# Routed experts of 128 tokens by gathered rows, with dense expert products of 384 columns

## The chip, the cores and the metric

The kernel runs on one core of a Trainium2 chip. The metric is the time of one execution on the device in microseconds, the median of several runs. Beside it stands one execution taken by the hardware profiler, whose trace gives every duration below.

## What is computed

One block with attention and a layer of routed experts (`peer`), then two blocks of another kind. The change touches `peer` alone. It has 512 tokens of width 1024, 16384 experts of one row each (`peer_u`, `peer_v`), eight heads that choose 16 experts for each token:

```
s1, i1 = lax.top_k(s[:, :, 0], K)
s2, i2 = lax.top_k(s[:, :, 1], K)
cand = (s1[..., :, None] + s2[..., None, :]).reshape(T, H, K * K)
sc, ci = lax.top_k(cand, K)
e1 = jnp.take_along_axis(i1, ci // K, axis=-1)
e2 = jnp.take_along_axis(i2, ci % K, axis=-1)
idx = e1 * PEER_NKEYS + e2
g = jax.nn.softmax(sc, axis=-1)
...
a = jnp.einsum('cd,chkd->chk', xc, u[ic])
act = (jax.nn.gelu(a.astype(jnp.float32)) * gc).astype(xc.dtype)
return jnp.einsum('chk,chkd->cd', act, v[ic])
```

So each token needs 128 rows of `u` and 128 rows of `v`.

## The kernel before

Most tokens are done densely: for all 128 groups of 128 experts (called experts in the loops) TensorE multiplies the group's tile of `u` with the tokens' features, the activations are masked with a matrix G of gate values, and products with `v` add them up. Every f32 product is three products in the f32r type (`mm3`, lines 177 to 179): weights and tokens are split into a high and a low part. The weight stream `WS.load` brings a tile of 128 x 1024 numbers over SyncE's queue, ScalarE casts it to `wh` (line 99), and VectorE or GpSimd subtracts to get `wl` (line 100). Three tiles of each kind are kept.

The first `TG` = 64 tokens are done by rows instead: GpSimd issues indirect DMAs that bring one row to each of 128 partitions (64 tokens, two halves of their choices), 64 gathers of `u` and 64 of `v`, each 512 KB (line 1373). VectorE multiplies the `u` rows with the tokens and sums (line 1390), later weights and adds the `v` rows into `av` (line 1409). The dense products have 512 - 64 = 448 columns.

`peer` runs in this order. The first loop goes over 128 up-experts, 24 products each. Beside it run generators, advanced by credits: `route` picks the experts, tile by tile of 128 tokens (four tiles), on VectorE: maxima and indices of scores, then sums of candidates, then lookups of the chosen indices by comparing with 0 to 15, multiplying and reducing (lines 1503 to 1507). ScalarE makes the Exp of `ge` (line 1488). When routing has ended, `build_g` makes G in steps of eight tokens: marks in f16 on VectorE (lines 1529 to 1535), 16 products of 128 columns on TensorE (line 1552), a scaled copy on ScalarE, and stores to DRAM as `g_d`. One `u` gather goes with each expert from there on. GpSimd makes `wl` for experts below `RES` = 104, VectorE for the others. The activations of experts below `RES` go to DRAM (`a_d`), the others stay in SBUF.

The second loop goes over the 128 down-experts: load G (`gt`) and activations (`at`), multiply (line 1319), split into `ah` and `al` (lines 215, 216), 24 products into eight PSUM banks `v`. VectorE makes all `wl`. The `v` gathers run beside it, with four row tiles. The last three experts' products are put off to a tail, after which two products of 64 columns for each bank fold `av` in.

TensorE's instructions in the first loop, and the `u` gathers, are held to program order (`keep_in_program_order`); a planner orders the rest for each engine. All engines run their own queue in order. A credit is about a microsecond and a half of VectorE's work in `route` and a step in `build_g`.

## Time and profile before

| | us |
|---|---|
| median of 3 runs | 3810.53 |
| lowest, highest | 3807.4, 3816.54 |
| profiled execution, its own time | 3815.04 |
| span of its trace | 3813.3 |
| TensorE busy in the span | 3712.7 (97%) |
| VectorE busy | 2128.6 (56%) |
| ScalarE busy | 1434.0 (38%) |
| GpSimd busy | 678.3 (18%) |
| mean granted TensorE clock | 0.979 of 2.4 GHz |

Busy times are shares of the whole span; matmuls overlap, so a busy TensorE is not one at its peak. What a stage is worth is read from that stage: a table by stretch shows busy time, number of instructions, granted clock, the busy share of the 16 DMA engines and the bytes moved. In the trace's names PE is TensorE, PEld its weight loads, DVE VectorE, ACT ScalarE, POOL GpSimd. The expert layer takes the time from about 600 to 2017 us of the span; the two blocks behind it last to the end.

### The profile page before, as it was taken

The page shows a single profiled execution, that of the slowest core. Times are in us where ns is not written, and L with a number is a line of the kernel's source. Part 1 is how long each engine was busy: PE and PEld are TensorE (multiplying, and loading weights), DVE is VectorE, ACT ScalarE, POOL GpSimd, SP SyncE. Part 2 cuts the span into 40 slices and gives each one's busy share as a digit, 9 for nine tenths or more (in the row PEclk, how much of TensorE's full clock was granted, in tenths as well). Part 3 has the DMA queues.
Part 4 walks back from the last instruction along what each step waited for, and adds up shares of the span by engine and source line. Part 5 has one row for each costly group of instructions (what it writes and reads, how often), then busy time and mean ns, then how long its engine had stood idle before and what let it go on. Part 6 is the DMA issues. An engine that isn't in the chain of part 4 may idle for free.

```text
span 3813.3 us, 46424 instructions
## 1 busy us (share of the span) xinstructions
PE 3712.7 (97%) x17947; PEld 3083.4 (81%) x17947; DVE 2128.6 (56%) x3507; ACT 1434.0 (38%) x2174; POOL 678.3 (18%) x407
## 2 busy tenths in 40 slices
PE   8999999998999999999999999999999999999998
PEld 7876568887888999999997866778887876878887
DVE  4436555993899658644446364454434554455333
ACT  4444433332566433333333444233223344333222
POOL 1000101454556425100000000121101000022100
PEclk9999899999999999999999999999999999999999
DMA  3124022443678878765553332532233233443232
GB/s 122 56 80 162 18 93 99 144 143 131 247 286 303 324 250 319 269 206 201 204 183 126 115 110 94 189 120 100 95 113 113 89 127 99 139 146 114 99 118 76
DMA packets 208022, 574.12 MB, mean 151 GB/s; under 512 B 20324, under 2 KB 53800, under 8 KB 207800
## 3 DMA queue, kind: packets, MB, share of 16 engines
q1 hardware_dynamic: 189336, 504.00, 38.7%
q0 software_dynamic: 18464, 67.15, 4.9%
q8 instruction: 141, 2.31, 0.2%
q14 instruction: 81, 0.66, 0.1%
HBM read 480.07 MB, written 90.96 MB: 150 GB/s over the span
## 4 chain that ended last, share of the span: by engine, by line
PE 57%; DVE 2%; DMA 2%; issue 1%; POOL 1%; ACT 1%; DVEq 0%; POOLq 0%
PE ps L177 13%; PE ps L179 13%; PE ps L178 13%; PE v L178 4%; PE v L177 4%; PE v L179 4%; DMA nv<-in_vr,gx 2%; PE o L414 1%; PE s L391 1%; PE pss L243 1%; PE tp L408 1%; POOL nv L1373 1%; PE o L773 0%; DVE xk L364 0%; PE bc L261 0%
## 5 line engine op out<-in xcount | busy, mean ns | idle before, releaser
L99 ACT CAST wh<-wr 128x1024 fp32r<-128x1024 f32 x599 | 629.7, 1052 | 1572.6 <-PE ps L178 816.0
L177 PE MATMUL ps<-hnh,wh 128*128 128x512 f32 (+1 forms) x2616 | 1017.7, 392 | 29.7 <-ACT hnh L316 16.0
L179 PE MATMUL ps<-hnh,wl 128*128 128x512 f32 (+1 forms) x2616 | 1011.7, 387 | 7.2 <-POOL wl L100 7.1
L178 PE MATMUL ps<-hnl,wh 128*128 128x512 f32 (+1 forms) x2616 | 1009.8, 386 | 0.0
L100 DVE TENSOR_TENSOR wl<-wr,wh 128x1024 fp32r<-128x1024 f32 x485 | 600.8, 1239 | 666.4 <-ACT wh L99 655.3
L177 PEld LDWEIGHTS ps<-hnh,wh 128*128 128x128 f32 x2616 | 499.3, 191 | 119.1 <-ACT hnh L316 17.0
L179 PEld LDWEIGHTS ps<-hnh,wl 128*128 128x128 f32 x2616 | 497.1, 190 | 95.7 <-POOL wl L100 8.5
L178 PEld LDWEIGHTS ps<-hnl,wh 128*128 128x128 f32 x2616 | 497.3, 190 | 82.2 <-DVE hnl L320 1.7
L100 POOL TENSOR_TENSOR wl<-wr,wh 128x1024 fp32r<-128x1024 f32 x114 | 305.8, 2688 | 533.4 <-ACT wh L99 519.6
L178 PE MATMUL v<-al,wh 128*128 128x448 f32 x1024 | 375.5, 367 | 2.2 <-DVE al L216 2.2
L179 PE MATMUL v<-ah,wl 128*128 128x448 f32 x1024 | 371.5, 363 | 0.0
L177 PE MATMUL v<-ah,wh 128*128 128x448 f32 x1024 | 370.8, 363 | 0.0
L178 PEld LDWEIGHTS v<-al,wh 128*128 128x128 f32 x1024 | 192.1, 188 | 17.1 <-DVE al L216 3.2
L177 PEld LDWEIGHTS v<-ah,wh 128*128 128x128 f32 x1024 | 191.8, 187 | 17.3
L179 PEld LDWEIGHTS v<-ah,wl 128*128 128x128 f32 x1024 | 192.2, 188 | 13.7
L674 POOL TENSOR_TENSOR sg<-sg,bcs 128x512 f32<-128x512 f32 x44 | 75.3, 1712 | 378.4 <-ACT sg L673 378.1
L1554 ACT ACTIVATE gs<-pg 128x512 f32<-128x512 f32 x112 | 120.7, 1193 | 44.3 <-PE pg L1552 44.3
L178 PE MATMUL ps<-hl,wh 128*128 128x512 f32 x352 | 137.0, 389 | 0.0
L177 PE MATMUL ps<-hh,wh 128*128 128x512 f32 x352 | 137.0, 389 | 0.0
L179 PE MATMUL ps<-hh,wl 128*128 128x512 f32 x352 | 137.0, 389 | 0.0
L237 POOL TENSOR_TENSOR sqa<-sqa,sq 128x512 f32<-128x512 f32 x30 | 45.8, 1527 | 510.2 <-DMA xd<-xk 476.1
L177 PE MATMUL ps<-wh,hnh 128*128 128x512 f32 (+1 forms) x320 | 126.2, 398 | 6.6 <-ACT hnh L316 6.6
(492 smaller groups left out, 5289.3 us busy)
## 6 DMA issues: line engine op xcount, KB each, us to landing
wr<-in_pu SPq DMA_DIRECT2D x128, 512.0 KB, 3.7
wr<-in_pv SPq DMA_DIRECT2D x125, 512.0 KB, 3.6
wr<-in_wgu SPq DMA_DIRECT2D x88, 512.0 KB, 3.4
g_d<-gs SPq DMA_DIRECT2D x64, 448.0 KB, 5.9
gt<-g_d SPq DMA_DIRECT2D x32, 896.0 KB, 5.8
wr<-in_wgate SPq DMA_DIRECT2D x48, 512.0 KB, 3.6
a_d<-ga SPq DMA_DIRECT2D x52, 448.0 KB, 3.5
at<-a_d SPq DMA_DIRECT2D x52, 448.0 KB, 4.5
```

Of the source, the lines that this page charges most:

```text
L99: nc.scalar.copy(hi, raw)
L100: eng.tensor_tensor(lo, raw, hi.bitcast(F32), OP.subtract)
L177: self.pe(nc.tensor.matmul(out, w[0], x[0], start=start, stop=False))
L178: self.pe(nc.tensor.matmul(out, w[0], x[1], start=False, stop=False))
L179: self.pe(nc.tensor.matmul(out, w[1], x[0], start=False, stop=stop))
L237: (eng or nc.vector).tensor_tensor(parts[0], parts[0], sq, OP.add)
L243: m = self.nc.tensor.matmul(p[:, i * NT + t:i * NT + t + 1], a, self.ones[:, 0:1], start=j == 0, stop=j == len(parts) - 1)
L391: nc.tensor.matmul(s[:, 0:n], q[:, t * P:n], k[:, 0:n], start=i == 0, stop=False)
L408: nc.tensor.transpose(tp[:, (t - b) * P:(t - b + 1) * P], pr[j, t][:, b * P:(b + 1) * P], self.ident)
L414: nc.tensor.matmul(o[j * 64:j * 64 + 64, b * P:S], heads[j][1](b), pts[j], start=first and b == 0, stop=last and b == NT - 1)
L674: nc.gpsimd.tensor_tensor(t, t, bc, OP.mult)
L1554: nc.scalar.mul(gs[:, :, t0 + h:t0 + h + 4].rearrange("p e t -> p t e"), p, 1.0 / GS)
```

## The change

`TG` becomes 128: the whole first tile of 128 tokens is done by rows, one token to a partition, 128 gathers of `u` and 128 of `v`. The dense products have 384 columns, and `build_g` has 48 steps in place of 56. The tables for the gathers are ready after the first routed tile, and the gathers run from there in one stream (`gather`, 260 steps: fetch, and four steps later the product) through both loops, paced by `NU_C` for each up-expert (0.4 while routing, 0.7 while `build_g` runs, 2.0 after) and `NV_C` = 1.35 for each down-expert, with six row tiles. All are held to program order. In the first loop GpSimd makes `wl` of every expert, in the second of every other one. Routing looks indices up in f16: comparing and multiplying 2048 elements as before, then four halving adds in place of a reduction. The Exp of `ge` comes after the first lookup and is held to program order. 112 experts' activations in place of 104 go through DRAM. Credits for an expert: 3.2 in routing (of 41 for a tile, 45 before, with 3.4), 0.85 in `build_g` (1.3 before).

```diff
@@ setup_late
-        self.ii = cp.tile([P, TG], F32, name="ii")
-        nc.vector.tensor_tensor(self.ii, self.ident[:, 0:TG], self.ident[:, TG:P], OP.add)
+        self.fold = []
+        for n in GROUPS:
+            if n == P:
+                self.fold.append(self.ident)
+                continue
...
@@ peer
-        xt = hp.tile([P, D], F32, name="xt")
+        xts = [hp.tile([P, D], F32, name=f"xt{n}") for n in GROUPS]
...
-        for i in range(2):
-            p = self.ps(name="xt")
-            for k in range(4):
-                for h in range(2):
-                    nc.tensor.matmul(p[h * TG:h * TG + TG, k * P:k * P + P], xs[4 * i + k][:, 0:TG],
-                                     self.ident, start=True, stop=True)
-            nc.scalar.copy(xt[:, i * S:i * S + S], p)
+        for i, (n, b0, _) in enumerate(group_cols()):
+            for j in range(2):
+                p = self.ps(name="xt")
+                for k in range(4):
+                    nc.tensor.matmul(p[0:n, k * P:k * P + P], xs[4 * j + k][:, b0:b0 + n], self.ident, start=True,
+                                     stop=True)
+                for q in range(0, P, n):
+                    nc.scalar.copy(xts[i][q:q + n, j * S:j * S + S], p[0:n])
...
-        near = self.gather_u(vp, sp, xt)
+        near = self.gather(vp, xts)
+        self.near_ready = False
...
-            wu.eng = nc.gpsimd if e < RES else nc.vector
+            wu.eng = nc.gpsimd
             wu.prefetch(2)
...
             else:
-                next(near, None)
                 credit += BG_C
+            if self.near_ready:
+                ncredit += NU_C[0 if not routed else 1 if gen is not None else 2]
+                while ncredit >= 1.0:
+                    next(near)
+                    ncredit -= 1.0
...
+            wv.eng = nc.gpsimd if n % 2 else nc.vector
+            wv.prefetch(2)
+            ncredit += NV_C
+            while ncredit >= 1.0:
+                next(near, None)
+                ncredit -= 1.0
             if n < P - VT:
                 for d in range(KD):
                     self.mm3(dense[d], wv.next(), (ah, al), n == 0, False)
-                if n % 5 and not far and next(near, None) is None and n >= P - RES:
-                    es.close()
-                    vq = self.pool(es, "near")
-                    av = vq.tile([P, D], F32, name="av")
-                    near = self.gather_v(vq, av)
-                    far = True
-                elif far and n % 5:
-                    next(near, None)
...
-            nc.tensor.matmul(acc[d][:, 0:TG], av[:, d * P:d * P + P], self.ii, start=False, stop=True)
+            for i, (m, b0, _) in enumerate(group_cols()):
+                nc.tensor.matmul(acc[d][:, b0:b0 + m], self.near_v[i][:, d * P:d * P + P], self.fold[i], start=False,
+                                 stop=b0 + m == TG)
...
+    def near_tables(self, vp, qp, em, ge):
+        nc = self.nc
+        nt = vp.tile([P, 2, TG], F32, name="nt")
+        whole = GROUPS == (P,)
+        gf = nt if whole else qp.tile([P, 2, P], F32, tag="cd", name="gf", bufs=1)
+        nc.vector.scalar_tensor_tensor(gf[:, 0], em[:, 0], float(P), em[:, 1], OP.mult, OP.add)
+        nc.vector.tensor_copy(gf[:, 1], ge.rearrange("p h k -> p (h k)"))
...
         self.near_i = vp.tile([P, TG], I32, name="gx")
+        nc.vector.tensor_copy(self.near_i, nt[:, 0])
+        self.near_g = nt[:, 1]
+        self.near_ready = True
+
+    def gather(self, vp, xts):
...
+        def fetch(src, j):
+            w = vp.tile([P, D], F32, tag="nr", name="nr", bufs=NR)
+            i = nc.gpsimd.indirect_dma_start(
+                out=w[:], out_offset=None, in_=self.a[src],
+                in_offset=bass.IndirectOffsetOnAxis(ap=self.near_i[:, j:j + 1], axis=0))
             self.tc.keep_in_program_order(i)
+            return w
         rows = []
+        for n in range(2 * TG + NL):
+            if n < 2 * TG:
+                rows.append(fetch("ur" if n < TG else "vr", n % TG))
+            j = n - NL
+            if 0 <= j < TG:
                 u = rows.pop(0)
+                nc.vector.scalar_tensor_tensor(u, u, 1.0, xts[group[j]], OP.mult, OP.mult, accum_out=a[:, j:j + 1])
+                if j == TG - 1:
+                    nc.scalar.activation(a, a, AF.Gelu_apprx_tanh)
+                    nc.vector.tensor_tensor(a, a, self.near_g, OP.mult)
+            elif j >= TG:
+                j -= TG
+                w = rows.pop(0)
...
+                    nc.vector.scalar_tensor_tensor(av, w, a[:, j:j + 1], av, OP.mult, OP.add)
             yield 1
...
@@ route
-                tf = qp.tile([P, 8, 2, 16], F32, tag="tf", name="tf", bufs=1)
-                nc.vector.tensor_copy(tf, ti)
+                tf = qp.tile([P, 2, 16, 8, 2], F16, tag="tf", name="tf", bufs=1)
+                for c in range(2):
+                    nc.vector.tensor_copy(tf[:, c], ti[:, :, c].rearrange("p h i -> p i h").unsqueeze(3)
+                                          .to_broadcast([P, 16, 8, 2]))
...
                 nc.vector.tensor_tensor(ge, cv, cv[:, :, 0:1].to_broadcast([P, 8, 16]), OP.subtract)
-                nc.scalar.activation(ge, ge, AF.Exp)
-                nc.vector.reduce_sum(gs[:, 0], ge, axis=AX.X)
...
-                    oh = qp.tile([P, P, 16], F32, tag="cd", name="oh", bufs=1)
-                    nc.vector.tensor_tensor(oh, fx.unsqueeze(2).to_broadcast([P, P, 16]),
-                                            io[:, 0:16].unsqueeze(1).to_broadcast([P, P, 16]), OP.is_equal)
-                    o4 = oh.rearrange("p (h k) i -> p h k i", h=8)
-                    nc.vector.tensor_tensor(o4, o4, tf[:, :, c].unsqueeze(2).to_broadcast([P, 8, 16, 16]), OP.mult)
-                    nc.vector.reduce_sum(em[:, c], oh, axis=AX.X)
-                    yield 7.0
+                    oh = qp.tile([P, 16, P], F16, tag="cd", name="oh", bufs=1)
+                    shape = [P, 16, P // 2, 2]
+                    nc.vector.tensor_tensor(
+                        oh.rearrange("p i (b u) -> p i b u", u=2),
+                        fx.rearrange("p (b u) -> p b u", u=2).unsqueeze(1).to_broadcast(shape),
+                        ior[:, 0:16].unsqueeze(2).to_broadcast(shape), OP.is_equal)
+                    o4 = oh.rearrange("p i (h k u) -> p (i h) k u", h=8, u=2)
+                    nc.vector.tensor_tensor(o4, o4, tf[:, c].rearrange("p i h u -> p (i h) u").unsqueeze(2)
+                                            .to_broadcast([P, P, 8, 2]), OP.mult)
+                    yield 3.0
+                    for n in (8, 4, 2, 1):
+                        nc.vector.tensor_tensor(oh[:, 0:n] if n > 1 else em[:, c:c + 1], oh[:, 0:n], oh[:, n:2 * n],
+                                                OP.add)
+                    yield 2.0
+                    if c == 0:
+                        self.tc.keep_in_program_order(nc.scalar.activation(ge, ge, AF.Exp))
+                nc.vector.reduce_sum(gs[:, 0], ge, axis=AX.X)
...
@@ constants
-TG = 64
+TG = 128
-RES = 104
+RES = 112
-RT_D = 12.0
-RT_C = 3.4
-BG_C = 1.3
+GROUPS = (128,)
+NR = 6
+NL = 4
+RT_D = 8.0
+RT_C = 3.2
+BG_C = 0.85
+NU_C = (0.4, 0.7, 2.0)
+NV_C = 1.35
```

## Rows read from the trace of the kernel before

**Rows 1.** Busy time by stretch: stretch, length, PE, PEld, DVE, ACT, POOL, clock, DMA share, GB/s.
```profile
655.00:958.00 303.00, 285.68 (x1404) 261.54 (x1403) 240.72 (x836) 100.83 (x141) 147.81 (x55) 0.97 0.40 139
958.00:1311.00 353.00, 339.04 (x2253) 304.78 (x2252) 311.58 (x349) 204.02 (x230) 196.92 (x104) 0.98 0.80 290
1311.00:1391.00 80.00, 80.00 (x396) 74.17 (x395) 44.90 (x61) 24.93 (x35) 10.61 (x8) 1.00 0.65 224
1391.00:2017.00 626.00, 623.81 (x3090) 577.74 (x3089) 355.93 (x418) 193.43 (x255) 88.06 (x66) 1.00 0.67 234
```
**Rows 2.** By stretch, line 178 alone: stretch, length, PE, PEld, clock, DMA.
```profile
655.00:958.00 303.00, 170.08 (x465) 88.80 (x465) 0.97 0.40 139
958.00:1311.00 353.00, 166.50 (x451) 86.26 (x451) 0.98 0.80 290
```
**Rows 3.** Timeline of PE, start and duration: down-products, first and last of 61.
```profile
1699.82 0.36 PE L177 MATMUL v<-ah,wh 128*128 128x448 f32 x1
...
1711.96 0.36 PE L177 MATMUL v<-ah,wh 128*128 128x448 f32 x1
```
**Rows 4.** By stretch, columns as in rows 1: a stretch of 512-column products alone.
```profile
2700.00:2800.00 100.00, 100.00 (x443) 82.82 (x442) 37.91 (x42) 29.67 (x37) 13.97 (x8) 1.00 0.33 112
```
**Rows 5.** Timeline of PE and PEld: products of 256 columns, first and last of 16.
```profile
45.02 0.28 PE L177 MATMUL ps<-wh,hnh 128*128 128x256 f32 x1
...
46.80 0.28 PE L177 MATMUL ps<-wh,hnh 128*128 128x256 f32 x1
...
45.15 0.19 PEld L179 LDWEIGHTS ps<-wh,hnl 128*128 128x128 f32 x1
```
**Rows 6.** By stretch, line 1552 alone, columns as in rows 2.
```profile
958.00:1311.00 353.00, 64.24 (x896) 52.67 (x896) 0.98 0.80 290
```
**Rows 7.** Groups of VectorE, 600 to 2010 us: busy us, mean ns, idle before.
```profile
L1506 DVE TENSOR_TENSOR oh<-oh,tf 128x2048 f32<-128x2048 f32 x8 | 23.1, 2882 | 0.1
L1503 DVE TENSOR_TENSOR oh<-fx,io 128x2048 f32<-128x2048 f32 x8 | 23.0, 2872 | 0.1
L1507 DVE TENSOR_REDUCE em<-oh 128x128 f32<-128x2048 f32 x8 | 18.2, 2273 | 0.1
L1461 DVE MATCH_REPLACE8 rs<-tv,rs 128x128 f32<-128x128 f32 x64 | 17.0, 274 | 0.0
```
**Rows 8.** The f16 marks: their group, and min/median/max in ns.
```profile
L1535 DVE TENSOR_TENSOR og<-e,gT 128x1024 f16<-128x1024 f16 x112 | 125.8, 1135 | 10.4 <-PE pg L1552 8.3
...
L1535 DVE TENSOR_TENSOR og<-e,gT x112: 676/685/3301, 967.7 to 1253.8; 128x1024 f16<-128x1024 f16 x112
```
**Rows 9.** Groups of VectorE, 600 to 2010 us: the row products.
```profile
L1390 DVE SCALAR_TENSOR_TENSOR nu<-nu,xt 128x1024 f32<-128x1024 f32 x64 | 83.9, 1313 | 10.2 <-DMA nu<-in_ur,gx 10.2
...
L1390 DVE DVE_READ_ACCUMULATOR nu<-nu,xt 128x1 f32 x64 | 5.1, 80 | 0.0
```
**Rows 10.** Waits of ScalarE, 655 to 960 us: total us, times, longest us.
```profile
ACT ge L1488 <- DVE ge L1487: 46.9, 4, 20.3
```
**Rows 11.** Line 100, the `wl` on either engine: min/median/max in ns.
```profile
L100 DVE TENSOR_TENSOR wl<-wr,wh x485: 1149/1225/2305, 5.9 to 3780.2; 128x1024 fp32r<-128x1024 f32 x162
...
L100 POOL TENSOR_TENSOR wl<-wr,wh x114: 2342/2410/4447, 641.7 to 3427.1; 128x1024 fp32r<-128x1024 f32 x114
```
**Rows 12.** The gathers on GpSimd: their group, and one behind another in the timeline.
```profile
L1373 POOL DMA_INDIRECT nv<-in_vr,gx x64 | 87.9, 1373 | 126.9 <-DVE av L1409 58.1 <-PE ps L179 57.0 <-DMA nv<-in_vr,gx 6.6
...
1443.10 0.94 POOL L1373 DMA_INDIRECT nv<-in_vr,gx  x1 [0.30 <-issue]
```
**Rows 13.** Groups of VectorE, 600 to 2010 us: activations times G.
```profile
L1319 DVE TENSOR_TENSOR at<-at,gt 128x448 f32<-128x448 f32 x104 | 60.1, 619 | 16.5 <-DMA at<-a_d 8.3 <-issue 5.1 <-DMA gt<-g_d 3.0
```
**Rows 14.** DMA issues of the page: count, KB each, us to landing.
```profile
gt<-g_d SPq DMA_DIRECT2D x32, 896.0 KB, 5.8
...
at<-a_d SPq DMA_DIRECT2D x52, 448.0 KB, 4.5
```
**Rows 15.** By stretch, columns as in rows 1: the busiest DMA.
```profile
1400.00:1500.00 100.00, 100.00 (x496) 92.74 (x495) 86.85 (x83) 31.84 (x42) 57.71 (x42) 1.00 0.93 334
```

More of the change, by code (lines that the diff above doesn't have):

```diff
@@ L1256, in peer @@
         gT = rp.tile([P, 2, S], F16, name="gT")
-        io = rp.tile([P, 16], F32, name="io")
+        io = sp.tile([P, 16], F32, name="io")
         nc.sync.dma_start(io, self.a["iota"])
@@ L1308, in peer @@
         tail = []
-        far = False
         for n, e in enumerate(V_SEQ):
@@ new lines, in near_tables @@
+        nc.vector.tensor_copy(gf[:, 1], ge.rearrange("p h k -> p (h k)"))
+        if not whole:
+            for n, b0, c0 in group_cols():
+                for q in range(P // n):
+                    nc.gpsimd.dma_start(nt[q * n:q * n + n, :, c0:c0 + n], gf[b0:b0 + n, :, q * n:q * n + n])
+        self.near_i = vp.tile([P, TG], I32, name="gx")
+        nc.vector.tensor_copy(self.near_i, nt[:, 0])
[3 more added lines that the diff above has]
+        nc = self.nc
+        a = vp.tile([P, TG], F32, name="na")
+        group = [i for i, n in enumerate(GROUPS) for _ in range(n)]
+        self.near_v = []
+        def fetch(src, j):
[3 more added lines that the diff above has]
+                in_offset=bass.IndirectOffsetOnAxis(ap=self.near_i[:, j:j + 1], axis=0))
@@ L1377, in gather @@
             self.tc.keep_in_program_order(i)
-    def gather_u(self, vp, sp, xt):
-        nc = self.nc
-        self.near_a = vp.tile([P, TG], F32, name="na")
+            return w
         rows = []
-        for j in range(TG + 2):
-            if j < TG:
-                u = sp.tile([P, D], F32, tag="nu", name="nu", bufs=3)
-                self.gather(u, "ur", j, True)
-                rows.append(u)
-            if j > 1:
-                u = rows.pop(0)
-                nc.vector.scalar_tensor_tensor(u, u, 1.0, xt, OP.mult, OP.mult,
-                                               accum_out=self.near_a[:, j - 2:j - 1])
-            yield 1
@@ L1394, in gather_v @@
-    def gather_v(self, vq, av):
-        nc = self.nc
-        a = self.near_a
-        nc.scalar.activation(a, a, AF.Gelu_apprx_tanh)
-        nc.vector.tensor_tensor(a, a, self.near_g, OP.mult)
-        rows = []
-        for j in range(TG + 2):
-            if j < TG:
-                w = vq.tile([P, D], F32, tag="nv", name="nv", bufs=4)
-                self.gather(w, "vr", j)
-                rows.append(w)
-            i = j - 2
-            if i == 0:
-                nc.vector.tensor_scalar(av, rows.pop(0), a[:, 0:1], None, OP.mult)
-            elif i > 0:
-                nc.vector.scalar_tensor_tensor(av, rows.pop(0), a[:, i:i + 1], av, OP.mult, OP.add)
-            yield 1
@@ L1413, in route @@
+    def route(self, hn, eT, gT, ior, vp):
         tc, nc = self.tc, self.nc
@@ L1512, in route @@
+                last = (t, em, ge) if t * P + P > TG else None
                 s = nxt
@@ L1569, with group_cols @@
 EG = 4
-RES = 104
+RES = 112
 NG = NS // NB
 VT = 3
-RT_D = 12.0
-RT_C = 3.4
-BG_C = 1.3
-V_SEQ = list(range(RES, P)) + list(range(RES))
+GROUPS = (128,)
[6 more added lines that the diff above has]
+NV_C = 1.35
+V_SEQ = list(range(RES, P)) + list(range(RES))
+def group_cols():
+    out, b = [], 0
+    for n in GROUPS:
+        out.append((n, b, b))
+        b += n
+    return out
 V_E16 = 0
```

50 lines of the change are left out of this document (22 added, 28 removed).

## The prediction

> **What bounds the kernel now.** The views were read in this order: busy time by stretch, then what one dense product costs, then what the other engines do in the same stretches. I cut the feed-forward part into four stretches: routing beside the first dense experts (655 to 958 us), the marks of `build_g` beside the next ones (958 to 1311), the last up-experts (1311 to 1391), and all down-products (1391 to 2017). TensorE is busy for 285.7 of 303, 339.0 of 353, 80.0 of 80 and 623.8 of 626 us [rows 1]; the reader is to see that it is the bound in the last two, nearly so in the second, and that some 17 us are lost in the first. The instructions of line 178, a third of the products, give the experts in each: (465 - 24 of the scores)/8 = 55.1, then 56.4 [rows 2]; of the 128 the rest, 16.5, is left for the third stretch, and the fourth has all 128 again. So all four stretches together hold 256 experts of 24 products, 6144 in all, and last 1362 us.
>
> A dense product of 448 columns follows the one before it after (1711.96 - 1699.82)/60 = 202.3 ns [rows 3]; one of 512 columns after 100 us/443 = 225.7 ns [rows 4]; one of 256 columns after (46.80 - 45.02)/15 = 118.7 ns [rows 5]. That is what a product costs; the mean duration of about 365 ns overlaps its neighbours.
>
> **The change, part by part.**
>
> *Narrower dense products, 448 to 384 columns.* Between 256 and 512 columns, 384 lies halfway: 172.2 ns. Between 256 and 448 it lies at two thirds: 118.7 + 0.667 x 83.6 = 174.4 ns. I take 174, so an expert falls from 24 x 202.3 = 4.86 us to 4.18 us. Over 6144 products the whole prize is 6144 x 28.3 ns = 174 us. `build_g` has 48 steps in place of 56, 768 f16 products in place of 896: 64.24/896 = 72 ns each [rows 6], so 9 us less. What decides is how much of it the other engines let TensorE have, stretch by stretch.
>
> *Routing stretch.* By the credits in the loop, near_tables is made at expert 12 and routing ends at expert 53: 54 experts. TensorE needs 54 x 4.18 + 10 (three score tiles of 24 products at 118.7 ns and the transposes) = 236 us. VectorE is busy for 240.7 us there now [rows 1]. Off it come the f32 lookups, 8 x (2872 + 2882 + 2273) ns = 64 us [rows 7]. On it come 16 f16 operations of 2048 elements and 32 adds. An f16 operation of 1024 elements takes 685 ns at the median and 3301 at worst [rows 8], one of f32 1225 [rows 11]: the double rate of f16 is in this trace. The mean of its group is 1135 ns, some 0.45 us of being held up. So 2048 elements take 1.2 + 0.5 us; the four adds take 0.68 + 0.42 + 0.28 + 0.28 (274 ns is what 128 elements cost [rows 7]) and about 0.5 of being held up: 16 x 1.7 + 8 x 2.2 = 45 us. The two f16 copies of `tf` per tile add about 2 us in all, the simpler tables give back 4 us. Then 16 row products at 1313 + 80 ns that used to come after routing [rows 9]: 22 us. Sum: 240.7 - 64 + 45 - 2 + 22 = 242 us. So VectorE and TensorE are nearly level, and the stretch is bounded by VectorE. Now ScalarE waits 46.9 us in four times, 20.3 at worst, for VectorE ahead of the Exp of `ge` [rows 10], with the weight casts `wh` queued behind it on ScalarE and TensorE behind those: most of the 17 lost us. The Exp moves behind the first lookup and is held to program order, which gives VectorE 5 credits, 1.6 experts or 7 us, more. I take 242 plus 10 of remaining mismatch: 252 us. Bounds: 240 (perfect overlap) and 275 (no double rate for the lookups, 16 x 1.1 us, and 5 of blocking).
>
> *Marks stretch.* Experts 53 to 110, 57 of them, at 0.85 step each. TensorE: 57 x 4.18 + 768 x 72 ns = 238 + 55 = 293 us. VectorE: 48 steps x 4 operations x 1.135 us = 218 us, and 40 row products x 1.39 = 56: 274 us. It was 311.6 of 353 [rows 1]. GpSimd: 57 x 2.41 + 40 gathers x 1.67 (both below) = 204 us. Both stay under TensorE. Before, TensorE's own need was 56.4 x 4.86 + 64 = 338 of 353. I keep 10 of those 15 us: 303 us; bounds 293 and 320.
>
> *Last up-experts.* Here two row reads go with each expert and GpSimd makes every `wl`. Undisturbed a `wl` takes it 2.41 us [rows 11]; a gather 1.37 us and 0.30 us of issue behind it [rows 11, 12]. That is 2.41 + 2 x 1.67 = 5.75 us for an expert, over the 4.18 of TensorE. GpSimd's queue is in order: a `wl` behind two gathers is late, and the third product of each triple waits for it. For 16 experts 92 us against 67. Some gathers can slip into the next stretch, where GpSimd has room. I take 84 for the 17 experts; bounds 71 and 95 (before: 80).
>
> *Down-products.* TensorE needs 3072 x 174 ns = 535 us. Of 260 steps of the row stream 89 are done by then; 168 of the 256 gathers are still to come. GpSimd: 64 x 2.41 + 168 x 1.67 = 435 us. VectorE: 128 x 2 operations on 384 columns at 0.56 us (619 ns at 448 [rows 13], less 64 elements at the 1.2 ns of [rows 11]) = 139 to 143, 64 `wl` at 1.22 = 78, 168 row products at 1.31 = 220: 441 us. Both fit. The DMA does not: 168 gathers and 128 weight tiles of 512 KB, 56 loads `at` of 384 KB, 32 of `gt` of 768 KB (sizes of now [rows 14] times 384/448) are 198,000 KB or 202 MB. The busiest stretch of the trace moved 334 GB/s at a share of 0.93 [rows 15], which is 358 GB/s at full share. 202 MB at 358 GB/s take 565 us, at 334 GB/s 606. TensorE was busy for all of those 100 us, so the load by itself did no harm; but there the gathers could be late without harm, and here their products stand in VectorE's queue ahead of `al`, which TensorE needs. I take 570 us; bounds 537 and 606. Before: 626. The last gather is issued at expert 123 and its product stands at 126; the 72 products put off to the tail, 12.5 us, hide it. If gathers lag by more, the sum in `av` ends the stretch instead, a few us inside the bounds.
>
> *At nothing.* Larger fold products at the end (16 records in both), and 16 fewer records of the `xt` transposes before 655 us: I count 2 us gained. Stores and reloads of 8 more experts are in the DMA sum.
>
> *Sum.* 252 + 303 + 84 + 570 = 1209 us in place of 1362: 153, and 2 more, less. The profiled execution took 3815.0 us (span 3813.3), so 3660; it lies 4.5 us above the median of the runs, which makes 3656 us. Low ends: 240 + 293 + 71 + 537 = 1141, so 3588. High ends: 275 + 320 + 95 + 606 = 1296, so 3743.
>
> **A rule weighed.** The f16 marks of one shape take from 676 to 3301 ns [rows 8], while GpSimd's `wl` takes 2342 at least [rows 11]; the longest mark is longer than the shortest by 2625 ns, about one such operation: VectorE is held up for one `wl`. The Trainium skill, page "SBUF — State Buffer", section "SBUF: two separate sides", has the reason: VectorE with two SBUF inputs and GpSimd share one port pair, held for a whole instruction, and the loser stops. The trace agrees with its lengths. By that rule the change is in trouble where it gives `wl` to GpSimd, which is the second rival below.
>
> **The rivals.**
>
> *TensorE stays the bound everywhere* (DMA and GpSimd keep up): the low ends, about 3590 us. For it: bursts are hidden by three weight buffers and six row buffers; against it: 202 MB in 535 us would be 378 GB/s, more than the busiest 100 us show.
>
> *VectorE and GpSimd exclude each other fully.* Then their undisturbed times add. Marks: 192 x 0.685 + 40 x 1.22 + 57 x 2.41 = 318 us. Down: 441 + 64 x 2.41 = 595 us. With 252 and 91: 1256 us, so 3702. Before, in the marks stretch the same sum was 224 x 0.685 + 56 x 1.22 + 48 x 2.41 + 10 = 347 of 353 us, which neither proves nor excludes it.
>
> *Gathers that wait hold the `wl` behind them (slower than before).* A gather waits on GpSimd's queue for its row buffer, and that for a product on VectorE. Now this wait is (58.1 + 6.6)/64 = 1.0 us a gather [rows 12], with no `wl` behind it. In the down stretch an expert takes GpSimd 1.2 + 1.35 x (1.67 + w): at w = 1.0 that is 4.8 us or 615 for the stretch (3701 in all), and from w = 1.7 it is 5.75 us, 736 for the stretch, and the kernel is slower than before; at w = 2.0 it takes 3874. Against it: six buffers in place of four, and gathers are spread by the credits.
>
> *Narrower products do not pay*, because the weight load of 0.19 us [rows 5] with some 12 ns between two is the real 202.3. Then TensorE gives nothing: 276 + 342 + 88 + 626 = 1332, so 3779. Against it: the same loads stand behind the products of 256 columns, and they come every 118.7 ns. If the f16 lookups alone fail to run at double rate, 3679.
>
> **How the numbers follow.** Forecast 3656 (from 3625 to 3690): 0.55. TensorE-bound, 3590 to 3625: 0.19. Exclusion, about 3702: 0.16. Gathers block: 0.05, of which 0.04 slower. No gain from width: 0.03. Lookups: 0.02. A difference of 0.2% is about what can be told here. Slower 0.04, within it 0.01, faster 0.95. The range leaves out the slow case, the widthless one and the outermost of the bounds: 3592 to 3740 us.
>
> **What would show it.** Right: 384-column products every 172 to 176 ns; ScalarE's wait ahead of Exp under 20 us; about 252, 303, 84 and 570 us in the stretches that end with experts 53, 110 and 127 and with the fold; DMA share above 0.9 through the down-products, with TensorE waiting on `al` or `wh`. Wrong: a DMA share well under 0.9 while TensorE idles behind `wl` on GpSimd, routing over 275 us, or a cadence above 180 ns.

## The result, and the profile after

The changed kernel takes 3685.32 us in the median of four runs (3677.55 to 3689.05), against 3810.92 for the kernel before, measured beside it: a ratio of 0.9666, with a 95% interval of 0.9647 to 0.9686. The prediction said 3656, in a range of 3592 to 3740. The profiled execution took 3677.55 us, its span 3675.8; it is the lowest of its four runs, while that of before lay above its median.

The stretches of the forecast can be laid over every kernel by the starts of the activations of experts 0, 54 and 110, the last of the up-experts, and the end of the last product into `v`. The first mark lies some 6 us behind the point at which the prediction begins its first stretch, and the second 4 us behind the end of expert 53, where the prediction ends it (in after, the activations of experts 53 and 54 start at 899.2 and 903.3 us). On the prediction's own marks routing took 253 us and the marks of `build_g` 297.

| us | routing | marks | last up-experts | down | sum |
|---|---|---|---|---|---|
| before | 296.8 | 352.9 | 80.9 | 625.0 | 1355.6 |
| forecast | 252 (from 6 us earlier, to 4 us earlier) | 303 (from 4 us earlier) | 84 | 570 | 1209 |
| after | 251.3 | 292.6 | 93.5 | 595.0 | 1232.4 |

Busy time of after by stretch, columns as in [rows 1]:

```profile
645.00:903.00 258.00, 244.80 (x1411) 243.65 (x1410) 256.90 (x904) 100.03 (x142) 160.94 (x73) 0.97 0.57 190
903.00:1196.00 293.00, 286.12 (x2116) 274.58 (x2116) 287.65 (x269) 179.47 (x210) 205.36 (x96) 1.00 0.82 286
1196.00:1289.00 93.00, 77.33 (x402) 73.16 (x401) 56.86 (x74) 24.88 (x37) 74.18 (x44) 0.94 0.93 330
1289.00:1885.00 596.00, 551.64 (x3090) 539.05 (x3089) 548.25 (x539) 188.69 (x259) 390.72 (x234) 0.99 0.93 339
```

Compare [rows 1]: TensorE filled the last two stretches before; now it lacks 16 us in one and 44 in the other. VectorE is busy for 257 of 258 us in routing and 548 of 596 in the down loop (355.9 before). The DMA share of the down loop went from 0.67 to 0.93.

The timeline of TensorE in the down loop, start and duration, first and last of 12 products:

```profile
1320.02 0.34 PE L185 MATMUL v<-ah,wl 128*128 128x384 f32 x1
...
1321.93 0.34 PE L183 MATMUL v<-ah,wh 128*128 128x384 f32 x1
```

(1321.93 - 1320.02)/11 = 173.6 ns, against 202.3 before [rows 3]. So the narrower product pays in full wherever TensorE is let run. The waits of the down loop in after, for TensorE, for ScalarE, and for SyncE's queue (us in total, times, longest):

```profile
PE v L183 <- ACT wh L99: 43.7, 35, 6.1
```
```profile
ACT ah L221 <- DVE at L1332: 265.8, 44, 7.2
```
```profile
SPq L91 <- DVE wl L100: 171.6, 68, 6.7
SPq L1329 <- DVE al L222: 160.7, 46, 7.1
SPq L91 <- POOL wl L100: 83.4, 27, 6.6
```

TensorE waits for `wh`. ScalarE, which makes `wh`, stands at `ah` of another expert and waits for VectorE's product `at`. SyncE's one queue brings weights (line 91) and stored activations (line 1329), and stands for a free buffer of either.

ScalarE's wait ahead of the Exp, 46.9 us [rows 10], is no longer among the waits of routing.

### The profile page after: what moved, and what is told of

It reads as the page before. It is cut to its first block, busy times and chain, and to the rows that moved or that the text cites. A ratio compares the mean times of both kernels' runs of the same rounds, so it can differ in the third digit from the quotient of the medians.

```text
span 3675.8 us, 46650 instructions
## 1 busy us (share of the span) xinstructions
PE 3534.8 (96%) x17800; PEld 2993.5 (81%) x17800; DVE 2316.4 (63%) x3605; ACT 1399.8 (38%) x2156; POOL 1067.1 (29%) x619
## 4 chain that ended last, share of the span: by engine, by line
PE 74%; DVE 18%; issue 3%; DMA 2%; ACT 2%; POOL 1%; SPq 0%; ACTq 0%; DVEq 0%; POOLq 0%
PE ps L183 18%; PE ps L185 18%; PE ps L184 17%; PE v L183 4%; PE v L184 3%; PE v L185 3%; DVE og L1559 3%; DVE nr L1409 2%; PE o L420 2%; PE s L397 2%; DVE e L1553 2%; DMA wr<-in_pv 1%; PE tp L414 1%; ACT wh L99 1%; DVE e L1555 1%
## 5 line engine op out<-in xcount | busy, mean ns | idle before, releaser
L100 DVE TENSOR_TENSOR wl<-wr,wh 128x1024 fp32r<-128x1024 f32 x400 | 499.5, 1249 | 415.0 <-ACT wh L99 408.9
L100 POOL TENSOR_TENSOR wl<-wr,wh 128x1024 fp32r<-128x1024 f32 x199 | 523.5, 2633 | 585.6 <-ACT wh L99 547.5
L183 PE MATMUL v<-ah,wh 128*128 128x384 f32 x1024 | 350.7, 343 | 43.7 <-ACT wh L99 43.7
L184 PE MATMUL v<-al,wh 128*128 128x384 f32 x1024 | 346.6, 339 | 0.0
L185 PE MATMUL v<-ah,wl 128*128 128x384 f32 x1024 | 229.0, 337 | 0.0
L1409 DVE SCALAR_TENSOR_TENSOR nr<-nr,xt 128x1024 f32<-128x1024 f32 x128 | 213.6, 1684 | 12.7 <-DMA nr<-in_ur,gx 12.7
L1423 DVE SCALAR_TENSOR_TENSOR av<-nr,na,av 128x1024 f32<-128x1024 f32 x127 | 209.5, 1650 | 1.6
L1397 POOL DMA_INDIRECT nr<-in_ur,gx x128 | 173.1, 1352 | 40.5 <-issue 11.9
L221 ACT CAST ah<-at 128x384 fp32r<-128x384 f32 x112 | 57.1, 512 | 324.5 <-DVE at L1332 265.8
L1397 POOL DMA_INDIRECT nr<-in_vr,gx x128 | 162.9, 1273 | 40.4 <-issue 19.1
```

Of the source, the lines that this page charges most:

```text
L100: eng.tensor_tensor(lo, raw, hi.bitcast(F32), OP.subtract)
L183: self.pe(nc.tensor.matmul(out, w[0], x[0], start=start, stop=False))
L184: self.pe(nc.tensor.matmul(out, w[0], x[1], start=False, stop=False))
L185: self.pe(nc.tensor.matmul(out, w[1], x[0], start=False, stop=stop))
L1397: i = nc.gpsimd.indirect_dma_start(out=w[:], out_offset=None, in_=self.a[src], in_offset=bass.IndirectOffsetOnAxis(ap=self.near_i[:, j:j + ...
L1409: nc.vector.scalar_tensor_tensor(u, u, 1.0, xts[group[j]], OP.mult, OP.mult, accum_out=a[:, j:j + 1])
```

## Experiments

All kernels start from the changed one. Their stretches by the marks above, in us (`rest` is the span outside the four: the code before and behind them is the same in all, and it varies by 9 us from one execution to another):

| | routing | marks | last up | down | rest | whole |
|---|---|---|---|---|---|---|
| after | 251.3 | 292.6 | 93.5 | 595.0 | 2443.4 | 3677.55 |
| e1_wide_up | 278.4 | 319.8 | 93.1 | 594.9 | 2442.8 | 3730.85 |
| e8_f32_lookups | 264.9 | 294.0 | 96.3 | 594.0 | 2451.7 | 3702.69 |
| e7_marks_wl_dve | 250.5 | 307.4 | 92.0 | 596.7 | 2449.0 | 3697.47 |
| e4_last_wl_dve | 250.6 | 293.2 | 87.2 | 598.1 | 2447.3 | 3678.14 |
| e2_short_rows | 255.0 | 289.1 | 93.6 | 609.0 | 2451.9 | 3700.27 |
| e3_short_products | 251.2 | 293.4 | 94.8 | 580.0 | 2444.5 | 3665.81 |
| e5_both_short | 255.0 | 291.4 | 93.4 | 613.5 | 2450.8 | 3705.74 |
| e6_down_wl_dve | 251.3 | 293.6 | 96.6 | 602.6 | 2446.4 | 3692.29 |
| e9_at_ahead | 250.5 | 292.8 | 96.2 | 589.8 | 2442.8 | 3674.04 |
| e10_raw5 | 250.5 | 292.9 | 106.4 | 618.9 | 2444.2 | 3714.64 |
| e11_all | 251.3 | 294.5 | 103.4 | 572.2 | 2450.4 | 3673.57 |
| e12_third | 251.3 | 293.1 | 102.5 | 567.7 | 2449.4 | 3665.81 |

All but e12 are one profiled execution each. Stretches that an edit leaves alone differ by up to some 5 us (routing from 250.5 to 255.0, the last up-experts from 92.0 to 96.6, the down loop from 594.0 to 598.1), so differences of 5 us or less in a stretch are not read.

In e10, e11 and e12 the mark between the last two stretches misleads: ScalarE casts weights of the down loop ahead of the last activations of the first loop, so the mark comes 7 to 9 us after TensorE's first product into `v`, where in after it comes 0.2 us after it. In e11:

```profile
1296.38 0.44 PE L184 MATMUL v<-ah,wh 128*128 128x384 f32 x1 [0.33 <-ACT wh L100]
```
```profile
1305.28 0.48 ACT L1310 ACTIVATE ar<-ps 128x384 f32<-128x384 f32 x1
```

From the first product into `v` to the last, the down loop takes 595.2 us in after, 590.0 in e9, 626.2 in e10, 581.1 in e11 and 575.1 in e12; the last up-experts, up to that product, take 93.3, 96.0, 99.1, 94.5 and 95.1.

### What the width gives in the first loop

```diff
-            p = self.ps("lin")[:, 0:NS]
+            pw = self.ps("lin")
+            p = pw[:, 64:64 + NS]
...
-                self.mm3(p, wu.next(), (hi[:, k, TG:], lo[:, k, TG:]), k == 0, k == KD - 1)
+                self.mm3(pw[:, 0:448], wu.next(), (hi[:, k, 64:], lo[:, k, 64:]), k == 0, k == KD - 1)
```

> The changed kernel, but the dense products of the first loop run over 448 columns again (64 of them are thrown away); everything else, VectorE's work above all, is as after the change. It splits the gain of the first loop into width and the rest. In the changed kernel routing beside experts 0 to 53 takes 251 us, the marks stretch to expert 110 takes 293, the last up-experts 93.5. If TensorE bounds a stretch, it grows by 24 x 27 ns = 0.65 us for each expert: routing to 286, marks to 329, the last to 94 to 97 (TensorE needs only 17 x 4.85 = 82 there). If VectorE bounds routing, as forecast, it grows only to what TensorE needs, 54 x 4.85 + 10 = 272 us; if it bounds the marks too (it is busy 288 of 293 us), these grow to TensorE's need of 57 x 4.85 + 55 = 331 all the same, since wider products then take the lead. Forecast: routing 274, marks 335, last 95, total longer by about 65 us.

Measured: 27.1 us more in routing, 27.2 in the marks, none in the last up-experts. That is 53 us in all, where 65 were expected; the marks came to 319.8 us and not to 335. Busy time of e1_wide_up, routing and marks, columns as in [rows 1]:

```profile
645.00:930.00 285.00, 281.31 (x1407) 259.53 (x1406) 253.65 (x900) 99.99 (x141) 155.73 (x73) 0.99 0.50 173
930.00:1249.00 319.00, 319.00 (x2109) 290.39 (x2107) 243.34 (x264) 178.22 (x208) 190.21 (x95) 1.00 0.73 261
```

With 448 columns TensorE is full in the marks (319 of 319) and nearly so in routing; with 384 VectorE is level with it. So of the 37 us that 54 experts could give (54 x 24 x 28.3 ns), routing kept 27, because VectorE's 257 us came next; the marks kept 27 of 38. The rest of the change brought 18 us in routing (296.8 - 278.4) and 33 in the marks (352.9 - 319.8). In the last up-experts width is worth nothing: another engine sets them.

### The f16 lookups

```diff
-                    oh = qp.tile([P, 16, P], F16, tag="cd", name="oh", bufs=1)
+                    oh = qp.tile([P, P, 16], F32, tag="cd", name="oh", bufs=1)
...
-                    for n in (8, 4, 2, 1):
-                        nc.vector.tensor_tensor(oh[:, 0:n] if n > 1 else em[:, c:c + 1], oh[:, 0:n], oh[:, n:2 * n],
-                                                OP.add)
+                    nc.vector.reduce_sum(em[:, c], oh, axis=AX.X)
```

> The changed kernel, but the lookups in routing are again f32 (comparing, multiplying and reducing 2048 elements), in the changed order, with Exp late. If VectorE bounds the routing stretch (busy 257 of 258 us), the stretch grows by what the lookups add, about 8 x (2.87 + 2.88 + 2.27) less 45 = 19 us, from 251 to 265 to 272 us. If TensorE or the late Exp set it, it stays within 5 us of 251.

Measured: routing 13.6 us longer, at the low end of what was expected, and VectorE busy for 264.6 of its 264.9 us (250.2 of 251.3 in after). So in routing VectorE's work sets the time.

### GpSimd's share of `wl` in the first loop

```diff
@@ e4_last_wl_dve
-            wu.eng = nc.gpsimd
+            wu.eng = nc.gpsimd if e < RES else nc.vector
@@ e7_marks_wl_dve
-            wu.eng = nc.gpsimd
+            wu.eng = nc.vector if routed and gen is not None else nc.gpsimd
```

> The changed kernel, but VectorE makes the low parts of the weights for the last 16 up-experts, as before the change. If GpSimd's queue bounds this stretch (93.5 us now; two gathers of 1.67 us and one low part of 2.4 us for each expert, TensorE waits 15 us for the low parts), it falls to 72 to 80 us. If the DMA does (share 0.93, 330 GB/s, 31 MB), it stays at 88 to 94 us, and TensorE waits for weights instead.

> The changed kernel, but while the marks run (experts 54 to 110) VectorE makes the low parts of the weights. VectorE is busy 288 of 293 us there with 56 low parts on GpSimd. If each of these holds VectorE up for some 2 us, its busy time falls to 192 x 0.685 + 40 x 1.3 + 56 x 1.25 = 254 us and the stretch stays at 285 to 293, bounded by TensorE (56 x 4.18 + 50). If it is not held up, VectorE would need 288 + 70 = 358 us and the stretch grows to 340 or more.

Measured: e4 shortens the last up-experts by 6.3 us, to 87.2. That is just under the range expected if the transfers set them (88 to 94) and far above the one for GpSimd's queue (72 to 80). Its stretch, columns as in [rows 1]:

```profile
1200.00:1287.00 87.00, 77.26 (x404) 74.80 (x404) 63.20 (x95) 23.83 (x36) 42.09 (x33) 0.92 1.01 376
```

GpSimd fell from 74.2 to 42.1 us, and the DMA is full at 376 GB/s: the transfers were next, 6 us behind GpSimd's queue. TensorE's waits there are 8.2 us for `wh` and 1.5 for `wl`, and ScalarE waits 9.7 us for weights to land.

In e7 VectorE's f16 marks run undisturbed and its busy time falls from 287.7 to 229.8 us, but the stretch is 14.8 us longer, between the two outcomes that were expected (285 to 293, or 340 and more). So ending the holding up in this way does not shorten the stretch. TensorE idles for 17 of its 307 us, where it was 7 of 293: it waits 9.0 us for the marks, 6.3 for `wh` and 2.0 for `wl`, and VectorE's `wl` wait 68.5 us for `wh` with the marks behind them in the queue. That this order costs the 14.8 us is likely, but no run shows it.

### The down loop: bytes, VectorE's work, or GpSimd's `wl`

e2 gathers rows of 256 numbers in place of 1024 for `v`, which VectorE reads four times over, so that its work stays; e3 gathers whole rows but weights 256 numbers of each; e5 does both; e6 gives every `wl` of the loop to VectorE.

```diff
@@ e2_short_rows, e5_both_short
-                out=w[:], out_offset=None, in_=self.a[src],
+                out=w[:] if src == "ur" else w[:, 0:256], out_offset=None,
+                in_=self.a[src] if src == "ur" else self.a[src].rearrange("e (q d) -> (e q) d", q=4),
...
@@ e3_short_products, e5_both_short
+                    av, w = av[:, 0:256], w[:, 0:256]
@@ e6_down_wl_dve
-            wv.eng = nc.gpsimd if n % 2 else nc.vector
+            wv.eng = nc.vector
```

> The changed kernel, but the 128 gathers of v rows bring 1 KB for each partition in place of 4 KB (a quarter of the row, of a quarter of the table), and VectorE reads that quarter four times, so its work is the same size. The sum over v rows is therefore another one. The DMA traffic of the down stretch falls from 202 MB to 152 MB; nothing else changes. If the DMA bounds this stretch (595 us now, at 345 GB/s and a share of 0.93 to 0.95), it falls to what TensorE needs, 535 to 550 us. If VectorE bounds it (busy 548 of 596 us, its row products stretched from 1.28 to 1.65 us by GpSimd's turns), it stays at 585 to 600 us.

> The changed kernel, but VectorE multiplies and adds only 256 of the 1024 columns of each v row (the other 768 columns of the sum are left at the first row's), while all rows are gathered in full. VectorE's work in the down stretch falls by 127 x 0.9 us or more, some 115 us of 548; the DMA traffic stays at 202 MB. If the DMA bounds the stretch, it stays at 580 to 595 us; if VectorE does, it falls to 535 to 555 us. If both experiments help in part, the two are coupled (loads wait for buffers that VectorE frees, and VectorE waits in turn).

> The changed kernel with both cuts at once: v rows of 1 KB for each partition, and products on 256 columns alone (the sum over v rows is another one). Short rows alone left the down stretch at 609 us (DMA share 0.71), short products alone at 580 us (VectorE busy 432 of 580, DMA share 0.95). Theory A, two bounds beside each other (DMA about 580, VectorE's queue about 600): with both cuts the stretch falls to TensorE's need, 535 to 550 us. Theory B, neither is the bound but the order of the queues (a weight cast on ScalarE behind a split that waits for VectorE or for TensorE; a load on SyncE's queue behind a weight tile that waits for its buffer): it stays at 570 to 600 us.

> The changed kernel, but VectorE makes the low parts of all down-expert weights, as before the change. If GpSimd's turn at a low part holds VectorE up for its whole length (2.4 us against the 1.25 us that VectorE needs itself), VectorE gains 62 x (2.0 - 1.25) = 45 us: its row products fall from 1650 ns to about 1300 and the down stretch from 595 to 565 to 585 us. If GpSimd's help is real help, VectorE's busy time rises from 548 by up to 62 x 1.25 = 77 us and the stretch to 620 or more.

Measured, down loop of e2, e3 and e5, columns as in [rows 1]:

```profile
1297.00:1907.00 610.00, 557.90 (x3091) 544.27 (x3089) 536.04 (x539) 191.44 (x258) 385.46 (x234) 0.99 0.71 250
```
```profile
1291.00:1871.00 580.00, 548.13 (x3089) 542.25 (x3088) 431.51 (x538) 191.11 (x258) 360.50 (x234) 0.99 0.95 348
```
```profile
1297.00:1910.00 613.00, 559.64 (x3086) 548.73 (x3085) 436.21 (x538) 190.97 (x257) 365.83 (x234) 0.98 0.70 248
```

Only e3 came out as one of the expectations had it, at the low end of the range for transfers: e2 took 609.0 us (535 to 550, or 585 to 600 expected), e3 580.0 (580 to 595, or 535 to 555), e5 613.5 (535 to 550, or 570 to 600) and e6 602.6 (565 to 585, or 620 and more). A quarter of the load off the DMA (0.93 to 0.71) shortened nothing; 117 us off VectorE gave 15; both at once gave a longer loop. Neither the sum of the transfers nor that of VectorE is the bound. In e2 TensorE waits 43.7 us for `al`, where in after it waited as long for `wh`: another queue is late, by the same amount.

e6, its loop cut where the gathers end:

```profile
1292.00:1722.00 430.00, 377.72 (x2088) 367.73 (x2087) 390.77 (x476) 131.17 (x176) 242.37 (x172) 0.98 1.01 385
1722.00:1895.00 173.00, 172.78 (x1003) 172.58 (x1001) 92.67 (x125) 60.75 (x82) 0.00 (x0) 1.00 0.64 214
```

With no `wl` on GpSimd the gathers run ahead and end 173 us before the loop does. Until then the DMA is full, at 385 GB/s, and TensorE is busy for 378 of 430 us; behind it TensorE runs without a gap. So here the transfers, bunched as they came, are the likely bound: ScalarE's `wh` waits 40.5 us for weights to land, 11.5 in after. The row products on VectorE, minimum, median and maximum in ns, in e6 and in after:

```profile
L1423 DVE SCALAR_TENSOR_TENSOR av<-nr,na,av x127: 1269/1280/1322, 1404.0 to 1722.8; 128x1024 f32<-128x1024 f32 x127
```
```profile
L1423 DVE SCALAR_TENSOR_TENSOR av<-nr,na,av x127: 1270/1280/3937, 1430.0 to 1875.9; 128x1024 f32<-128x1024 f32 x127
```

The same as groups, busy us and mean ns, in e6 and in after:

```profile
L1423 DVE SCALAR_TENSOR_TENSOR av<-nr,na,av 128x1024 f32<-128x1024 f32 x127 | 162.9, 1283 | 1.4
```
```profile
L1423 DVE SCALAR_TENSOR_TENSOR av<-nr,na,av 128x1024 f32<-128x1024 f32 x127 | 209.5, 1650 | 1.6
```

No row product is held up once GpSimd only gathers; with every other `wl` there, the mean rises by 367 ns. Over the whole loop VectorE is busy for 483.4 us in e6, though it makes 62 more `wl` at 1.22 us, and for 548.3 in after. So those 62 on GpSimd save VectorE 76 us and cost it 76 + 65 = 141 of being held up.

### The down loop: queues in order

e9 issues the loads of `at` four experts ahead; e10 gives the raw weight tiles of the loop five buffers; e11 does both, with e4's edit.

```diff
@@ e9_at_ahead, e11_all (AHEAD = 4)
...
-                at = vp.tile([P, 2, NS], F32, tag="at", name="at", bufs=2)
-                nc.sync.dma_start(at, a_d[e // 2])
+            for m in range(n, min(n + AHEAD + 1, P)):
+                f = V_SEQ[m]
+                if f < RES and f % 2 == 0 and f not in ats:
+                    ats[f] = vp.tile([P, 2, NS], F32, tag="at", name="at", bufs=2 + AHEAD // 2)
+                    nc.sync.dma_start(ats[f], a_d[f // 2])
...
@@ e10_raw5, e11_all
-            raw = wp.tile([P, PW], F32, tag="wr", name="wr", bufs=3)
+            raw = (self.rp or wp).tile([P, PW], F32, tag="wr", name="wr", bufs=5 if self.rp else 3)
...
+        wv.rp = vp
```

> The loads of the stored activations (`at`) are issued four experts earlier, with four buffers in place of two; nothing else changes. Theory A (in the down loop SyncE's loads of `at` stand behind a weight load that waits for a free buffer, so `ah`, and behind it on ScalarE the next `wh`, comes late): the down loop, 595 us in the changed kernel, falls to 570 to 582, ScalarE's wait for the product of `at` (265.8 us in 44) falls by more than half, and the whole run comes to 3655 to 3670. Theory B (the transfers themselves set the down loop, at a busy share of 0.93): it stays between 590 and 600, and ScalarE's wait stays or turns into a wait for `wr`. Theory C (VectorE's queue, two row products and a `wl` between one product of `at` and the next, sets the loop): also 590 to 600, with ScalarE still waiting for the product of `at`, and that product not waiting for its load.

> In the down loop the weight tiles as they come from memory (`wr`) have five buffers in place of three; `wh` and `wl` keep three. SyncE's waits for a `wl` to free a buffer (171.6 us in 68 waits on VectorE alone) should nearly go. Theory A (loads stuck behind a full buffer hold back `at` and `gt`, and the weights): the down loop falls from 595 us to 570 to 580. Theory B (transfers set the loop): 590 to 600, the busy share still 0.93. Theory C (VectorE's order sets it): 590 to 600, with the weights waiting in their buffers, and ScalarE waiting for the product of `at` as before.

> Three edits at once: `at` issued four experts ahead, five buffers for `wr` in the down loop, and `wl` of the last 24 up-experts made by VectorE in place of GpSimd. By theory A the down loop takes 560 to 575 us and the last up-experts 87: the run comes to 3640 to 3655. By theories B and C the down loop stays at 590 to 600, the last up-experts take 87, and the run comes to 3672 to 3684.

Measured: e9 589.8, e10 618.9, e11 572.2. What TensorE waits for in the loop, e9, e10, e11:

```profile
PE v L183 <- ACT wh L99: 38.6, 20, 6.3
```
```profile
PE v L184 <- ACT ah L222: 43.5, 28, 4.8
PE v L185 <- DVE al L223: 22.3, 26, 1.5
```
```profile
PE v L1361 <- DVE av L1431: 19.3, 1, 19.3
PE v L184 <- ACT wh L100: 7.8, 5, 1.6
PE v L186 <- POOL wl L101: 5.6, 8, 1.6
```

With `at` ahead ScalarE no longer waits for VectorE's product, and the weights are late as before: 5 us gained, no more than executions differ by. With more weight buffers the weights come ahead and the activations are late: 24 us lost by the marks, 31 from TensorE's first product into `v` to its last. With both, the waits inside the loop fall from 43.7 us to 13.4, but 19.3 us for the last row sums are new at its end. The loop is 23 us shorter by the marks, 14 from the first product to the last.

Theory A of these three expectations had the pair's loop right by the marks (572.2, for 560 to 575). It had neither edit alone right, nor the last up-experts of the pair (103.4 for 87), nor its run: 3673.57 us lies where theories B and C put it (3672 to 3684). No theory had e10's 618.9. The last two stretches of e11 together come to 675.6 us against 688.5, 13 less; e4's edit alone gives 685.3. What e4 gained in the last up-experts is gone in e11, where TensorE waits there for `wh`:

```profile
PE ps L184 <- ACT wh L100: 21.0, 4, 15.6
```

ScalarE waits 21.2 us for weights to land at this place (10.4 in after), at a DMA share of about 1.0. The early loads of `pv` weights are the likely reason; no run tests it.

### A better version

```diff
@@ e12_third (e11_all, and)
-            wv.eng = nc.gpsimd if n % 2 else nc.vector
+            wv.eng = nc.gpsimd if n % 3 == 2 else nc.vector
```

> As e11_all, but in the down loop GpSimd makes one `wl` in three in place of one in two. In e11_all the down loop took 572 us and ended with TensorE waiting 19.3 us for the last weighted `v` rows (the gathers, held up by `wl` work on GpSimd, ended late); in e6_down_wl_dve, with no `wl` on GpSimd, the gathers ended 170 us early at a DMA share of 1.00 to 1.04, and TensorE ran without a wait only after that. Theory D (three bounds close together: TensorE about 535 us, the transfers at 371 to 398 GB/s about 510 to 545, VectorE with its hold-ups 527; what counts is that the gathers last as long as the products): between the two the gathers end near the end of the loop, the wait for the last rows is under 5 us, the down loop comes to 545 to 565, and the run to 3640 to 3665, below the changed kernel's lowest. Rival (the early gathers take the weights' share of the DMA as in e6_down_wl_dve): the loop takes 572 to 595 with TensorE waiting for `wh` on `wr` in its first two thirds, and the run 3673 to 3690.

Measured in five rounds: 3665.81 us median (3664.96 to 3671.38), 0.9625 of before (0.9612 to 0.9638); its highest run lies below the lowest of the changed kernel, 3677.55. The down loop takes 567.7 us, 3 above what was expected (575.1 from the first product to the last), the run is 1 us above its range, and the last row sums still come late, where a wait under 5 us was expected:

```profile
PE v L1361 <- DVE av L1431: 17.0, 1, 17.0
PE v L184 <- ACT wh L100: 11.1, 7, 1.6
```

By this the balance of `wl` between the engines did little beside e11 (4.5 us in single executions, no more than they differ by). GpSimd's gathers wait 163 us for VectorE to free a row buffer there, so VectorE's order at the end of the loop is the next thing to try; neither that nor a faster pace of gathers was tried.

## Why the prediction was right, and where its steps were off

*The sum.* On the prediction's marks the stretches come to 253.1 + 296.7 + 93.5 + 595.0 = 1238 us, against 1209: 29 more. The code outside them took 14 us less than before, where 2 were counted. The trace shows why for most of it: the same instructions come 4.1 us earlier after the first 45 us and 8.5 us earlier by 450. In the first 100 us the granted clock was 0.97 before and 1.00 after, between 400 and 500 us 0.91 and 0.97. This is luck and no gain of the change: over the changed kernel and the experiments, whose code up to there is the same, the first activation of expert 0 starts anywhere from 650.7 to 659.9 us. The other 5 to 6 us lie mostly behind the expert layer and were not followed up. So the profiled execution came 17.6 us above the forecast of 3660. The medians lie 29 us apart, and the other 12 us are where each profiled execution stood to its median: 4.5 us above it before, 7.8 below it after. A forecast made against one execution carries that.

*Width.* Right: 174 ns forecast, 173.6 measured. The halfway rule between products of 256 and 512 columns held, and the rival by which the weight loads set the pace fell.

*Routing*, 252 forecast, 253 measured to the end of expert 53. VectorE as the bound was right: 252.7 of 253.8 us busy, and e8's 13.6 us arrive whole, a little under the 16 x 1.1 us that the prediction's bound names. The size of two terms was off: the groups of the lookups and of the row products in routing,

```profile
L1516 DVE TENSOR_TENSOR oh<-fx,ior 128x2048 f16<-128x2048 f16 x8 | 14.5, 1807 | 0.1
L1521 DVE TENSOR_TENSOR oh<-oh,tf 128x2048 f16<-128x2048 f16 x8 | 13.8, 1720 | 0.1
L1525 DVE TENSOR_TENSOR oh<-oh 128x1024 f16<-128x1024 f16 (+2 forms) x24 | 27.3, 1139 | 0.3
...
L1409 DVE SCALAR_TENSOR_TENSOR nr<-nr,xt 128x1024 f32<-128x1024 f32 x16 | 30.5, 1913 | 0.0
```

The comparisons and products took 28.3 us for the 27.2 forecast. The halving adds took 30 (with a group of 2.3 us for the last) for 17.6, and a row product 1.91 us for 1.31. Both were held up more than allowed: five of the 16 row products took 3.3 to 3.6 us, the others 1.2. VectorE's whole came to 253 us for 242; the 10 us added for "mismatch" with TensorE covered nearly all of that, for another reason than the one given. That the total fits to 1 us is luck.

*Marks*, 303 forecast, 297 measured for the same 57 experts. TensorE's need of 293 us was too large. In e1 TensorE has no gap in 319 us, which hold 1341 dense products of 202.3 ns and 768 of f16: that leaves 62 ns for one of f16 (an estimate) where 72 were counted, and 285 us for the need. So some 12 us were lost, where 10 were kept from before. VectorE, forecast at 274 us and under TensorE, was busy for 291 of the 297, level with it; the width could give 38 us and gave 27. The exclusion rival's 318 us fell here, and in e7 undisturbed marks did not shorten the stretch.

*Last up-experts*, 84 forecast, 93.5 measured. The working was right: GpSimd's queue gives 92 us for 16 experts. The discount to 84, for gathers that slip into the next stretch, was wrong: 42 gathers of `u` came in the down loop, where the forecast's own pace leaves 39, so about three slipped. TensorE's wait there in after:

```profile
PE ps L185 <- POOL wl L100: 15.3, 12, 2.7
```

That is the `wl` behind two gathers, as the prediction had it. What it left out stands close behind: without this queue (e4) the transfers hold the stretch at 87.2. A wait also costs more than its length. In one of 2.72 us TensorE's granted clock fell to half, 1.2 of 2.4 GHz, and for the next 6 us products came every 0.32 us in place of 0.17, which cost about 3 us more (an estimate from 19 such products):

```profile
1249.00:1255.00 6.00, 5.82 (x18) 5.82 (x19) 5.13 (x9) 0.00 (x0) 3.83 (x4) 0.50 0.73 251
```
```profile
1249.18 0.69 PE L185 MATMUL ps<-hnh,wl 128*128 128x384 f32 x1 [2.72 <-POOL wl L100]
1249.66 0.52 PE L183 MATMUL ps<-hnh,wh 128*128 128x384 f32 x1
1249.98 0.52 PE L184 MATMUL ps<-hnl,wh 128*128 128x384 f32 x1
```

*Down-products*, 570 forecast, 595 measured: the mis-sized term. The step that failed is "The DMA does not" fit. Its 202 MB were right (339 GB/s over 596 us). Its full-share rate of 358 GB/s, from 334 at a share of 0.93, was too low: e4 and e6 moved 376 and 385. At 385 the 202 MB take 525 us, below TensorE's 535. And with 0.71 of the share (e2) the loop is no shorter. What stood in its place, as far as e9, e10 and e11 show it, is two rings of buffers behind one another in queues that run in order (SyncE's loads, ScalarE's `ah` and `wh`): from the first product to the last, 590.0 and 626.2 us for either alone, 581.1 for both, 595.2 in after. Together they take TensorE's waits inside the loop from 43.7 us to 13.4, but only 14 us off the 60 us by which the loop exceeds TensorE's need; what sets the rest stays open. The sign named for the DMA term, a share above 0.9 with TensorE waiting on `wh`, came all the same, so it does not tell a full DMA from queues that wait in turn. VectorE's 441 us were also short by 107: the row products took 1.65 us and `al` 1.10 where 1.31 and 0.56 were counted.

*The exclusion rival* gave 595 us for the down loop, and 595 came. That does not make it the cause: the holding up is real (1283 and 1650 ns above), but where it is removed (e6) the loop takes 602.6, and where VectorE has 117 us less to do it takes 580. The Trainium skill, page "SBUF — State Buffer", section "SBUF: two separate sides", says that of a VectorE operation with two SBUF inputs and a GpSimd operation that reads SBUF, whichever starts first has the shared port pair for its whole instruction; e6's 1322 ns at most against 3937 agrees. How much of such holding up reaches the end of a stretch is another question: in routing, where VectorE has no gap, it does; in the marks (e7) and in the down loop (e6), moving `wl` off GpSimd did not shorten the stretch.

*The slow rival*, gathers that hold `wl` behind them: in the down loop the gathers waited 12.6 us in all for `av` buffers, 0.1 us each. It fell.

Left open: why shorter rows (e2, e5) make the loop 14 to 18 us longer, and why e7's marks stretch is. In e5 VectorE waits 143.8 us for `at` loads, so the order of loads is the nearest candidate; no run has short rows with `at` ahead.

## What to carry to other kernels

When a change relieves the engine that bounds a stretch, price the next bound by its queue, with everything that stands in it in order, and not by its sum of work: TensorE's need (535 us), VectorE's busy time (548) and the transfers (525) were each 88 to 92% of the loop here, and none of them alone set it. Where a loop waits on two rings of buffers in one queue, deepen both: here one alone gave 5 us or cost 31, and both together gave 14, from the first product of the loop to the last. Before counting an offload to GpSimd as VectorE's gain, count what it holds up: here 62 operations moved away saved 76 us and cost 141. And before removing such a cost, ask what it hides: without it (e6) the gathers came bunched, and the loop was not shorter. Take the marks of a stretch from the engine that the stretch is about: a mark on ScalarE moved by 7 to 9 us when the order of its work changed.

## What was not expected of the hardware

The transfers of this core reached 376 GB/s over 87 us (e4) and 385 over 430 us (e6), at a share of 1.01; a rate scaled up from a stretch at 0.93 gave 358. A single VectorE operation on f32 rows that takes 1.27 us took up to 3.94 us with GpSimd subtracting weights beside it, and never over 1.32 with GpSimd only gathering.
